# A decoder layer's opening stage: one norm block's parts and the next one's scaling in a fixed order, and other banks for even blocks

## The chip, the cores and the metric

The kernel runs on one core of a Trainium2 chip. The metric is device time in microseconds of one execution; the kernel before takes 1291.82 us (median of three runs, 1291.59 to 1291.99). The engines are named as in the profile: PE (TensorE, with PEld for its weight loads), DVE (VectorE), ACT (ScalarE), POOL (GpSimd) and SP (SyncE, which issues the DMAs here).

## The reference

One layer over 1040 tokens (16 meta tokens ahead of 1024) of width 1024, all in float32. What matters for the change is the beginning: RMSNorm of the input, then the combined input projection.

```python
h = jnp.concatenate([meta, x], axis=1)
a = rmsnorm(h, ln_mix_pre[l])            # h * rsqrt(mean(h*h) + 1e-6) * gain
proj = a @ w_in[l]
dq, dk, dv, hq, hf, hi, hg = jnp.split(proj, SPLITS, axis=-1)
```

Behind it come differential attention (four heads, two softmaxes each), HGRN2 (a gated linear recurrence), the output projection, a second norm and a feed-forward part with a short convolution. The change touches none of these.

## The kernel before, in words

Every matrix product is made of three: each operand is split into a high part (a cast to the rounded float32 that TensorE multiplies fast) and a low part (operand minus high part), and high times high, high times low and low times high are summed in PSUM.

**Norm blocks.** The tokens come in nine blocks of 128 rows (the last has 16). A block i goes through these steps:
- its rows are loaded into `xt` (`load_x`, four buffers, the first of which the gain row `grow` uses at the start);
- ACT squares them with a running sum into a score bank `pj` and makes the row factor `ss` with a logarithm and an exponential (`pre_stat`);
- DVE multiplies each half (512 columns) by the factor and the gains `gb` into `xs` (`pre_scale`, the SCALAR_TENSOR_TENSOR `xs<-xt,ss,gb`), here called scaling(i, half);
- PE transposes each half in four steps into a PSUM bank `px` (`pre_turn`, L292);
- ACT casts the bank to the high part (`pre_hi`, CAST `a<-px`) and DVE subtracts for the low part (`pre_lo`, TENSOR_TENSOR `a<-px,a`).

**PSUM.** Three tags have two buffers each: "ip" (one bank, the projections' sums `pi`), "m" (one bank, most transposes) and "S" (a pair of banks, the score tiles of attention, which the opening also uses). A transposition into an "m" bank waits until the low part of the half that had that bank is made. A projection's sum in an "ip" bank waits until the result before the last is evacuated: dv's first matmul waits for dq's evacuation, which is an ACT multiplication (`q<-pi_dq`) and then DVE's low part (`q<-pi_dq,q`, two instructions).

**Tokens and weights.** The projections of head 0 (dq, dk, dv) run over three token groups; the first needs blocks 0 and 1, the second blocks 2 to 4, the third blocks 5 to 8. Weights come in halves of 512 rows of the contraction. For dq and dk, ACT casts a half and POOL subtracts for its low part; for dv (tile `w`, called `third` in the code), DVE casts and POOL subtracts. Raw halves go through three buffers `wr`, so a fourth load waits until POOL has read the first.

**What sets the order.** PE's instructions stand as they are written. In the opening, ACT's and DVE's do too, as long as `state["ordered"]` is true (class `Ordered`): each instruction issued through `A` or `V` keeps its place in the program. After that a scheduler places them. SP's DMAs stand in one queue: a load that waits holds up those behind it. Norm work and projection are mixed by `interleave`: its side generator (`pre_blocks`) yields after each half block, and between two yields the dense generator gives PE a budget of matmuls; `lead` is the budget ahead of the first.

The ordered part ends, before, with block 2's scaling. Block 2's transposes and parts, block 3's scaling and dv's two casts follow in the scheduler's order.

## Time and profile before

| | |
|---|---|
| median of three runs | 1291.82 us (1291.59 to 1291.99) |
| the profiled execution | 1290.12 us |
| its span, first to last instruction | 1288.3 us |
| mean granted clock of PE | 0.997 |
| PE, DVE, ACT, POOL busy | 98%, 70%, 54%, 32% of the span |

The profile describes one execution. A row of its order in time gives start and duration in us, the engine, the line, the operation, the tile written and the tiles read; a bracket at the end gives the idle time of the engine before it and what ended that. Rows of many ACT and DVE instructions carry L57, the line of the helper that records them, so they are told apart by their tiles. Names are without numbers: `px` stands for all the transposes' banks. "x4" joins four equal instructions. The opening with the change ends at about 45 us.

### The profile page before, as it was taken

What the parts mean: (1) busy time and instruction counts of PE and PEld (TensorE: products, weight loads), DVE (VectorE), ACT (ScalarE), POOL (GpSimd) and SP (SyncE); (2) the same over time, 40 slices, a digit from 0 to 9 for tenths busy, and PEclk for the clock granted to TensorE, in tenths of its full rate; (3) what the DMA queues carried; (4) which work ended last, traced back from release to release, by engine and by line L of the source; (5) the groups of instructions that cost most, each with busy time, mean ns of one, the idle gap of its engine ahead of it and who ended that gap; (6) DMA issues with size and microseconds to landing.
All of it is one profiled execution on the core that took longest, in us unless ns stands there. A gap on an engine that the chain in (4) does not pass through costs nothing.

```text
span 1288.3 us, 26390 instructions
## 1 busy us (share of the span) xinstructions
PE 1268.2 (98%) x10264; PEld 1181.5 (92%) x10264; DVE 904.2 (70%) x1579; ACT 692.1 (54%) x1698; POOL 409.4 (32%) x322
## 2 busy tenths in 40 slices
PE   7999999999999999999999999999999999999997
PEld 7899999999999999777999999999999998888886
DVE  6576647564757476747797778778778786697587
ACT  7465357545654566446665445445445454454454
POOL 3221212021212110122165766766766730010120
PEclk9999999999999999999999999999999999999999
DMA  6222222212222223837512322222222237955363
GB/s 223 95 84 69 84 83 98 70 68 83 99 73 89 66 91 110 269 104 241 204 59 84 112 77 91 75 83 90 76 83 85 81 101 233 340 185 172 90 213 123
DMA packets 84387, 153.07 MB, mean 119 GB/s; under 512 B 9587, under 2 KB 19859, under 8 KB 84262
## 3 DMA queue, kind: packets, MB, share of 16 engines
q1 hardware_dynamic: 84262, 151.39, 35.4%
q8 instruction: 80, 1.31, 0.4%
q14 instruction: 45, 0.37, 0.1%
HBM read 112.69 MB, written 38.67 MB: 117 GB/s over the span
## 4 chain that ended last, share of the span: by engine, by line
PE 66%; DVE 2%; ACT 1%; DMA 0%; issue 0%; DVEq 0%
PE pd L1616 5%; PE pd L1615 5%; PE pd L1614 5%; PE pb L1415 4%; PE pb L1416 4%; PE pb L1417 4%; PE pa L1416 3%; PE pa L1417 3%; PE pa L1415 3%; PE pc L1416 3%; PE pc L1415 3%; PE pc L1417 3%; PE py L1030 2%; PE py L1034 2%; PE py L1032 2%; PE pq L1392 2%
## 5 line engine op out<-in xcount | busy, mean ns | idle before, releaser
L1415 PE MATMUL pb<-t,uh 128*128 128x258 f32 (+1 forms) x456 | 127.4, 279 | 0.6 <-DVE u L57 0.6
L1416 PE MATMUL pb<-t,uh 128*128 128x258 f32 (+1 forms) x456 | 127.3, 279 | 0.0
L1417 PE MATMUL pb<-t,ul 128*128 128x258 f32 (+1 forms) x456 | 127.2, 279 | 0.0
L1616 PE MATMUL pd<-wh,gl 128*128 128x512 f32 (+1 forms) x314 | 121.0, 386 | 0.0
L1615 PE MATMUL pd<-wl,gh 128*128 128x512 f32 (+1 forms) x314 | 120.5, 384 | 0.4 <-DVE wl L57 0.3
L1614 PE MATMUL pd<-wh,gh 128*128 128x512 f32 (+1 forms) x314 | 120.8, 385 | 0.0
L57 DVE SCALAR_TENSOR_TENSOR c<-uu,cwt,c 128x512 f32<-128x512 f32 x88 | 94.9, 1079 | 22.2 <-ACT c L57 21.4
L1364 POOL TENSOR_TENSOR c<-c,c 128x512 f32<-128x512 f32 x44 | 64.3, 1462 | 127.1 <-ACT c L57 112.9
L57 DVE SCALAR_TENSOR_TENSOR c<-ug,cwt,c 128x512 f32<-128x512 f32 x88 | 83.9, 954 | 6.6 <-ACT c L57 5.9
L1415 PEld LDWEIGHTS pb<-t,uh 128*128 128x128 f32 x456 | 85.8, 188 | 0.9 <-DVE u L57 0.8
L1416 PEld LDWEIGHTS pb<-t,uh 128*128 128x128 f32 x456 | 85.9, 188 | 0.0
L1417 PEld LDWEIGHTS pb<-t,ul 128*128 128x128 f32 x456 | 85.9, 188 | 0.0
L1416 PE MATMUL pa<-t,uh 128*128 128x256 f32 (+1 forms) x304 | 85.3, 281 | 0.0
L1417 PE MATMUL pa<-t,ul 128*128 128x256 f32 (+1 forms) x304 | 85.2, 280 | 0.0
L1415 PE MATMUL pa<-t,uh 128*128 128x256 f32 (+1 forms) x304 | 85.2, 280 | 0.0
L1417 PE MATMUL pc<-t,ul 128*128 128x256 f32 x304 | 83.9, 276 | 0.0
L1415 PE MATMUL pc<-t,uh 128*128 128x256 f32 x304 | 83.9, 276 | 0.0
L1416 PE MATMUL pc<-t,uh 128*128 128x256 f32 x304 | 83.9, 276 | 0.0
L1615 PEld LDWEIGHTS pd<-wl,gh 128*128 128x128 f32 x314 | 58.9, 188 | 14.0 <-DVE wl L57 1.5
L1616 PEld LDWEIGHTS pd<-wh,gl 128*128 128x128 f32 x314 | 59.0, 188 | 12.1
L1614 PEld LDWEIGHTS pd<-wh,gh 128*128 128x128 f32 x314 | 59.0, 188 | 11.6
L57 ACT ACTIVATE c<-ug,cbt,cwt 128x512 f32<-128x512 f32 x44 | 35.9, 817 | 44.0 <-issue 26.2
(421 smaller groups left out, 4278.2 us busy)
## 6 DMA issues: line engine op xcount, KB each, us to landing
ra<-in_wup_dram SPq DMA_DIRECT2D x76, 256.0 KB, 2.7
wd<-in_wdown_dram SPq DMA_DIRECT2D x44, 256.0 KB, 3.3
tsc<-wd SPq DMA_DIRECT2D x44, 256.0 KB, 2.5
gsc<-c SPq DMA_DIRECT2D x44, 256.0 KB, 2.0
wi<-tsc SPq DMA_DIRECT2D x44, 256.0 KB, 2.9
gi<-gsc SPq DMA_DIRECT2D x33, 256.0 KB, 4.0
wi<-in_wdown_dram SPq DMA_DIRECT2D x33, 256.0 KB, 3.7
msc<-mm SPq DMA_DIRECT2D x21, 256.0 KB, 3.6
```

Source lines behind the costliest of these rows:

```text
L57: ins = call(*args, **kw)
L1030: T.matmul(py[:r], mh[:, j, :r], hi, start=(first and j == 0), stop=False)
L1032: T.matmul(py[:r], mh[:, j, :r], lo, start=False, stop=False)
L1034: T.matmul(py[:r], ml[:, j, :r], hi, start=False, stop=(last and k == k1 - 1))
L1364: G.tensor_tensor(cg, cg, cu, op=ALU.mult)
L1392: T.matmul(pt, hi[:, s], th[:, k], start=(kh + k == 0), stop=False)
L1415: T.matmul(pt, hi[:, s], th[:, k], start=(first and k == 0), stop=False, skip_group_check=True)
L1416: T.matmul(pt, hi[:, s], tl[:, k], start=False, stop=False, skip_group_check=True)
L1417: T.matmul(pt, lo[:, s], th[:, k], start=False, stop=(k == 3), skip_group_check=True)
L1614: T.matmul(py, gh[:, s], wh, start=(k == 0 and pr not in (3, 7)), stop=False, skip_group_check=True)
L1615: T.matmul(py, gh[:, s], wl, start=False, stop=False, skip_group_check=True)
L1616: T.matmul(py, gl[:, s], wh, start=False, stop=(k == NH - 1), skip_group_check=True)
```

## The change

It does five things, all in the opening:
- the load of block 3 is issued ahead of the second half of dk's weights;
- block 2's transposes, high and low parts, dv's two casts with POOL's two subtractions, and block 3's scaling are written into the ordered part, with the matmuls that PE has between them;
- block 3's `xs` is made there, so `pre_block(3)` finds it ready;
- even blocks that remain (4, 6 and 8) transpose both halves into one pair of the "S" tag, instead of two "m" banks;
- the load of block 6 is issued by itself ahead of the interleaving, which now begins with block 3 and a lead of 700 instead of 2600.

```diff
@@ pre_block
         for half in range(2):
-            out_ = pre_turn(i, half, xs[:, 512 * half:])
+            if i % 2 == 0 and half == 0:
+                pair = ps_s(f"px{i}")
+            out_ = pre_turn(i, half, xs[:, 512 * half:], None if i % 2 else pair[:, half])
             pre_hi(*out_)
@@ opening
     keep_warm(4)
+    load_x(3)
     raws[1, 1] = load_raw(tiles[1][0], 1, tiles[1][1])
-    load_x(3)
     scale(0, 1)
@@ end of the ordered part
     scale(2, 1)
+    third = [ap_.tile([P, 4, 512], F32R, tag="pb", name=f"w3{c}", bufs=2) for c in range(2)]
+
+    def third_weights(c):
+        V.tensor_copy(third[c][:, 0], raws[2, c])
+        G.tensor_tensor(third[c][:, 1], raws[2, c], third[c][:, 0].bitcast(F32), op=ALU.subtract)
+
+    parts.append([(third[c][:, 0], third[c][:, 1]) for c in range(2)])
+    xss[3, 0] = zp.tile([P, D], F32, tag="xs", name="xs3")
+    xss[3, 1] = xss[3, 0][:, 512:]
+    for _ in range(22):
+        next(first_group)
+    h20 = pre_turn(2, 0, xss[2, 0])
+    third_weights(0)
+    scale(3, 0)
+    pre_hi(*h20)
+    pre_lo(*h20)
+    for _ in range(8):
+        next(first_group)
+    h21 = pre_turn(2, 1, xss[2, 1])
+    last_hi = pre_hi(*h21)
+    third_weights(1)
+    pre_lo(*h21)
+    scale(3, 1)
     xts.pop(2)
+    xts.pop(3)
     state["ordered"] = False
-    third = [ap_.tile([P, 4, 512], F32R, tag="pb", name=f"w3{c}", bufs=2) for c in range(2)]
-    parts.append([])
-    for c in range(2):
-        raw = raws[2, c]
-        with tc.issue_after(V.last.ins):
-            V.tensor_copy(third[c][:, 0], raw)
-            G.tensor_tensor(third[c][:, 1], raw, third[c][:, 0].bitcast(F32), op=ALU.subtract)
-        parts[2].append((third[c][:, 0], third[c][:, 1]))
@@ after the definitions
-    interleave(first_group, [pre_blocks([2, 3, 4])], 800, 2600)
+    load_x(6)
+    interleave(first_group, [pre_blocks([3, 4])], 800, 700)
```

On DVE, from block 2's second scaling (`xs_267`) to dq's low parts: a minus is a row of before, a plus one of the change. `xs_344` and `xs_283` are block 3's, `w_281` and `w_282` dv's two halves, `px_0` and `px_1` block 2's transposed halves, and `a_109` the low parts.

```order
 L57 SCALAR_TENSOR_TENSOR xs_267<-xt_154,ss_251,gb 128x512
-L57 SCALAR_TENSOR_TENSOR xs_344<-xt_219,ss_276,gb 128x512
 L57 CAST w_281<-wr_dv_0_235 128x512
-L57 SCALAR_TENSOR_TENSOR xs_344<-xt_219,ss_276,gb 128x512
+L57 SCALAR_TENSOR_TENSOR xs_283<-xt_217,ss_276,gb 128x512
+L57 TENSOR_TENSOR a_109<-px_0_306,a_108 128x4x128
 L57 CAST w_282<-wr_dv_1_244 128x512
-L57 TENSOR_TENSOR a_109<-px_0_310,a_108 128x4x128
 L57 TENSOR_TENSOR a_109<-px_1_324,a_108 128x4x128
+L57 SCALAR_TENSOR_TENSOR xs_283<-xt_217,ss_276,gb 128x512
 L57 SCALAR_TENSOR_TENSOR q_0_133<-pi_dq_0_162,q_0_133 64x256
 L57 SCALAR_TENSOR_TENSOR q_0_134<-pi_dq_0_162,q_0_134 64x256
```

Dv's first cast now stands ahead of scaling(3, 0), block 2's first low part ahead of the second cast, and scaling(3, 1) behind the second low part; dq's low parts stay behind all of it.

On ACT, from block 3's factor (`ss_276`) on: `px_0` and `px_1` are again block 2's halves, `pj_384` and `ss_385` block 4's squares and factor, `pj_459` block 5's squares.

```order
 L57 ACTIVATE ss_276<-ss_276 128x1
+L57 CAST a_108<-px_0_306 128x4x128
+L57 CAST a_108<-px_1_324 128x4x128
 L57 ACTIVATE pj_384,ss_385<-xt_222 128x1024
-L57 CAST a_108<-px_0_310 128x4x128
-L57 CAST a_108<-px_1_324 128x4x128
-L57 ACTIVATE ss_385<-ss_385,eps 128x1
 L57 ACTIVATE q_0_133<-pi_dq_0_162 64x256
 L57 ACTIVATE q_0_134<-pi_dq_0_162 64x256
-L57 ACTIVATE ss_385<-ss_385 128x1
-L57 ACTIVATE pj_459,ss_460<-xt_246 128x1024
```

Block 2's high parts moved ahead of block 4's squares, and block 4's factor behind dq's evacuation.

In SP's queue, at the second half of dk's weights (`wr_dk_1`): `xt_154` is block 2's load, `xt_219` and `xt_217` block 3's, `xt_222` block 4's.

```order
 L270 DMA xt_154<-in_x_dram 128x1024
-L810 DMA wr_dk_1_217<-in_win_dram 128x512
-L270 DMA xt_219<-in_x_dram 128x1024
+L270 DMA xt_217<-in_x_dram 128x1024
+L812 DMA wr_dk_1_219<-in_win_dram 128x512
 L270 DMA xt_222<-in_x_dram 128x1024
```

Block 3's load and dk's second half changed places; block 4's stays behind both.

## The prediction

> **What bounds the kernel now.** I read the page first, then the waits of TensorE (PE), then the order of time on each engine around the longest wait. The page says that PE is busy nearly throughout:

> ```profile
> span 1288.3 us, 26390 instructions
> ...
> PE 1268.2 (98%) x10264; PEld 1181.5 (92%) x10264; DVE 904.2 (70%) x1579; ACT 692.1 (54%) x1698; POOL 409.4 (32%) x322
> ```

> So a gain at one place stays if PE is then earlier for good. The waits of PE (total us, times, longest) have one long one:

> ```profile
> PE px L292 <- DVE a L57: 3.0, 1, 3.0
> ...
> PE pb L360 <- DVE a L57: 0.4, 1, 0.4
> ```

> The change touches the stage of the 3.0. On PE, in order of time (start us, us):

> ```profile
> 18.25 0.28 PE L896 MATMUL pi_dk<-a,wh_dk 128*128 128x256 f32 x1
> 21.51 0.82 PE L292 MATMUL px<-ident,xs 128*128 128x128 f32 x4 [2.98 <-DVE a L57]
> 21.99 0.99 PE L896 MATMUL pi_dk<-a,wh_dk 128*128 128x256 f32 x3
> 23.07 0.55 PE L249 MATMUL pi_dv<-a,w 128*128 128x256 f32 x1
> ...
> 28.34 0.34 PE L249 MATMUL pi_dq<-a,wh_dq 128*128 128x384 f32 x1
> ```

> Block 3's first transposes (21.51) stand in PE's queue ahead of ready matmuls. They write a bank of the pair "m" that block 2's first half still holds until its low part (DVE `a<-px,a`) is made. DVE makes that late:

> ```profile
> 15.33 1.60 DVE L57 SCALAR_TENSOR_TENSOR xs<-xt,ss,gb 128x512 f32<-128x512 f32 x1
> 17.71 0.75 DVE L57 SCALAR_TENSOR_TENSOR xs<-xt,ss,gb 128x512 f32<-128x512 f32 x1 [0.77 <-ACT ss L57]
> 18.38 0.42 DVE L57 CAST w<-wr_dv 128x512 fp32r<-128x512 f32 x1
> 18.71 0.74 DVE L57 SCALAR_TENSOR_TENSOR xs<-xt,ss,gb 128x512 f32<-128x512 f32 x1
> 19.37 1.48 DVE L57 CAST w<-wr_dv 128x512 fp32r<-128x512 f32 x1
> 20.78 1.27 DVE L57 TENSOR_TENSOR a<-px,a 128x512 fp32r<-128x512 f32 x2
> 22.07 0.86 DVE L57 SCALAR_TENSOR_TENSOR q<-pi_dq,q 64x256 fp32r<-64x256 f32 x2
> ```

> (In order: scaling(2,1), scaling(3,0), dv's first cast, scaling(3,1), its second cast, block 2's two low parts, the two q parts.) Two are longer than their kind: a scaling takes 0.75 but here 1.60, a cast 0.42 but here 1.48. Beside them POOL ran:

> ```profile
> 15.10 1.29 POOL L160 TENSOR_TENSOR wl_dk<-wr_dk,wh_dk 128x512 fp32r<-128x512 f32 x1 [0.96 <-ACT wh_dk L57]
> 18.87 1.70 POOL L924 TENSOR_TENSOR w<-wr_dv,w 128x512 fp32r<-128x512 f32 x1 [2.48 <-DVE w L57]
> 20.94 1.28 POOL L924 TENSOR_TENSOR w<-wr_dv,w 128x512 fp32r<-128x512 f32 x1 [0.36 <-DVE w L57]
> ```

> The scaling of 15.33 ends 0.54 after POOL's 16.39; the cast of 19.37 ends 0.28 after POOL's 20.57; POOL's own 1.70 began while the scaling of 18.71 ran. So DVE scalings and casts out of SBUF and POOL's subtractions exclude each other; the low parts, which read PSUM, do not.

> The stall has a second price. In stretches of one clock record, 3.41 us each (PE busy is the first number behind the comma, PEclk the third from the right, then DMA share and GB/s):

> ```profile
> 18.45:21.87 3.42, 0.44 (x4) 0.36 (x4) 3.42 (x6) 3.38 (x10) 2.63 (x2) 1.00 0.94 336
> 21.87:25.28 3.41, 3.31 (x16) 3.05 (x15) 3.32 (x7) 2.26 (x7) 0.35 (x1) 0.50 0.31 81
> 602.13:605.55 3.42, 2.75 (x14) 1.93 (x13) 3.42 (x4) 2.17 (x7) 1.50 (x1) 1.00 0.76 225
> 1281.39:1284.80 3.41, 0.49 (x5) 0.28 (x3) 3.25 (x7) 1.81 (x7) 0.00 (x0) 1.00 0.68 266
> 1284.80:1288.21 3.41, 0.00 (x0) 0.00 (x0) 0.58 (x1) 0.00 (x0) 0.00 (x0) 0.50 0.49 181
> ```

> A stretch with PE busy 0.44 or 0.49 of 3.41 us is followed by one at half clock. At 2.75 of 3.42 the kernel kept its clock.

> **The change part by part.** *Block 3's load ahead of dk's second half.* SP and ACT, before:

> ```profile
> 4.36 0.43 SPq L270 DMA_DIRECT2D xt<-in_x_dram  x1
> 11.21 0.33 SPq L810 DMA_DIRECT2D wr_dk<-in_win_dram  x1
> 11.64 0.85 SPq L270 DMA_DIRECT2D xt<-in_x_dram  x2
> ```
> ```profile
> 14.40 0.62 ACT L57 CAST wh_dk<-wr_dk 128x512 fp32r<-128x512 f32 x1
> 15.96 1.03 ACT L57 ACTIVATE pj<-xt 128x1024 f32<-128x1024 f32 x1 [0.94 <-DMA xt<-in_x_dram]
> ...
> 17.47 0.20 ACT L57 ACTIVATE ss<-ss 128x1 f32<-128x1 f32 x1
> ...
> 19.92 0.76 ACT L57 ACTIVATE q<-pi_dq 64x256 fp32r<-64x256 f32 x2
> ```
> ```profile
> 14.00:15.00 1.00, 1.00 (x10) 1.00 (x10) 0.94 (x2) 1.00 (x3) 0.14 (x1) 1.00 1.10 373
> 11.00:12.00 1.00, 1.00 (x8) 1.00 (x7) 1.00 (x2) 0.86 (x3) 1.00 (x2) 1.00 0.01 4
> ```

> The weight load at 11.21 had to wait for POOL; block 3's load stood behind it. Now that load goes out about 0.45 after 4.36, and the DMA engines that sat idle at 11 to 12 have it to move. The 0.94 before ACT's squares goes, and block 3's factor is ready at 17.67 - 1.0 = 16.7. Price: its 0.5 MB takes 1.4 us at 373 GB/s, estimated. It costs the weights nothing if it stays behind those issued ahead of it, up to 1.4 if it shares with them; I take nothing, since everything ahead is issued by then and it joins the end. The same 1.4 us are gained by dv's weights behind it: landed by 18.38 before, by 17.0 now (estimate; bounds 15.6, with the idle us and the start-up gained too, and 18.4).

> *The fixed order on DVE.* From scaling(2,1), whose end stays at 16.93:
> - dv's first cast 17.0 to 17.4, scaling(3,0) to 18.1 (0.75), block 2's first low part to 18.7 (half of 1.27).
> - Block 3's transposes start at 18.75, not 21.51: the 2.98 falls to about 0.4. PE then does three dk matmuls and is through at 19.6.
> - POOL's first subtraction, begun at 17.5, takes 1.70 beside a scaling as it did before: to 19.2. The second cast ends 0.28 later, 19.5; the second low part at 20.1.
> - POOL's second subtraction runs 19.55 to 20.85. Scaling(3,1), ready at 20.0, is now behind it: 20.85 + 0.54 = 21.4. Before, it was done at 19.45.
> - Queued behind it on DVE are the two q parts: 0.86, to 22.25.

> **What is late next** is those q parts. The first dv matmul takes the bank that dq's result leaves only then (there are two such banks). Before: parts done 22.93, matmul 23.07, 0.14 later. Now 22.25 + 0.14 = 22.4. PE waits 19.6 to 22.4, 2.8 us: the stall moves behind the transposes. Gain at this point 23.07 - 22.4 = 0.7.

> [...]

> *From the first dv matmul to 28.34*, where the second token group starts. In 18.45 to 21.87 PE now works 18.75 to 19.6 and the first 0.1, about 0.95 of 3.41 (28%). Whether that halves the clock is unmeasured: the bounds are 14% (halved) and 80% (not), and 28% is nearer the first. If halved, the slow stretch holds 25.28 - 22.4 = 2.9 us of work instead of 2.2, and each costs half: 0.35 of the 0.7 is lost, and the gain is about 0.4. If not, 2.2 / 2 = 1.1 more is gained: 1.8. DVE, busy over 97% of both rows, has block 4's scalings behind all this, so I take 1.7.

> *The pair of score banks* takes even blocks' waits for an "m" bank away. The only such wait of note was block 3's, which is odd: nothing here, and 0.4 at block 8 (the pb row) is the wait for the low part itself. Bounds: 0 and -0.4. *The fixed order on ACT* (block 2's high parts ahead of block 4's squares) is what gives the low part at 18.7; it costs nothing: the squares and the two high parts stood ahead of the q evacuation of 19.92 before as well, and block 3's factor, ahead of all three, is 1.0 earlier. Without that it would be the second low part that waits, and DVE is not at it before 19.4. *Later loads.* Block 7's load waits for scaling(3,1), now 21.4, behind three small tables on SP, where before the three of blocks 5 to 7 were out by 19.84:

> ```profile
> 14.54 5.30 SPq L270 DMA_DIRECT2D xt<-in_x_dram  x3
> ```
> ```profile
> 27.63 1.02 ACT L57 ACTIVATE pj<-xt 128x1024 f32<-128x1024 f32 x1
> ```

> Block 7's squares ran at 27.63: 6 us of cover. Without it, 1.9 us of delay would fall on block 7's transposes.

> Sum on the profiled execution: span 1288.3 - 0.4 = 1287.9, and the 1.8 around it (its time was 1290.12) gives 1289.7. That execution was 1.7 under the median of the runs, 1291.82; taken from the median, the forecast is 1291.4.

> **The rivals.**
> 1. *The clock stays up.* 28% busy suffices. For: nothing halved at 80%. Against: 13 and 14% did. Gain 1.7: 1290.1. [...]
> 2. *Slower: dv's weights land late.* The first cast now stands ahead of scaling(3,0) and the low part in fixed order, so every us of landing past 17.0 moves all of it. At the present landing, 18.4, dv's first matmul starts at 23.8, 0.7 later than now, and 0.35 of that comes back since less work falls into the slow stretch: 0.4 of loss, 1292.2. It decides from 17.7, where the 0.7 is used up. For: the cast at 18.38 started just when DVE and the weights allowed. Against: SP issues the same transfers earlier.
> 3. *The exclusion does not bite*: POOL's second subtraction starts after scaling(3,1). Then scaling(3,1) ends at 20.75, the q parts at 21.6, dv's first matmul starts at 21.75, 1.3 earlier; with the clock kept (1.1) and block 4's scalings earlier too (0.6) the gain is 3.0: 1288.8. Against: POOL began 0.1 after each cast before. The upper bound is stall and slow clock both gone, 3.0 + 1.7 = 4.7.

> **How the numbers follow.** Forecast 0.48, rival 1 0.27, rival 2 0.17, rival 3 0.08. The range 1289.7 to 1292.6 holds the forecast and rivals 1 and 2 with 0.4 of slack for the landing's bounds, and leaves out rival 3 and the tails. A measurement can tell 0.2%, 2.6 us, from no change. Only rival 3 passes it below: its 0.08, and 0.02 for what I don't see. Above, only rival 2 with more going wrong, 0.05. Within: 0.85.

> **What would show it.** Right: the wait of px for DVE `a` falls under 0.7, and a wait of 2 to 3 us stands before the first pi_dv matmul, at 22.4; one scaling of 1.3 us ends at about 21.4; PEclk 0.50 in 21.87 to 25.28. Wrong: dv's first matmul before 21.5 or after 23; a cast of w that waits for a DMA; or a new PE wait after 28 us, which would mean that the gain is not kept.

## The result, and the profile after

The changed kernel is slower: 1292.43 us (median of 22 executions, 1290.87 to 1298.29) against 1291.33 us for the kernel before beside it (22 executions, 1289.95 to 1294.35). The ratio is 1.0015, 95% interval [1.0009, 1.0022], so 0.15%, about 1.9 us; the two medians alone lie 1.1 us apart. The forecast was 0.4 us faster.

The profiled execution took 1293.35 us with a span of 1291.5, that is 3.2 more than the span before (1288.3). It lay 0.9 over its own median, and that of before 1.2 under the median of its 22. So the two profiles show more than the change costs as a rule, and the 3.2 is taken apart here with that in mind.

The waits of PE after (us in total, times, longest), the lines that answer to those of before:

```profile
PE pi_dv L249 <- DVE q L57: 2.7, 1, 2.7
...
PE px L292 <- DVE a L57: 1.0, 2, 0.6
...
PE pl L494 <- issue: 0.8, 1, 0.8
```

Of the 3.0 ahead of block 3's transposes 0.44 is left, and 2.7 stands before dv's first matmul. The line of `px` now holds two short waits, this one and one of 0.60 at block 8. The line of `pl` is new: a wait in which no semaphore is waited for. In order of time on PE:

```profile
19.23 0.66 PE L292 MATMUL px<-ident,xs 128*128 128x128 f32 x4 [0.44 <-DVE a L57]
19.64 0.60 PE L898 MATMUL pi_dk<-a,wh_dk 128*128 128x256 f32 x3
22.92 0.55 PE L249 MATMUL pi_dv<-a,w 128*128 128x256 f32 x1 [2.68 <-DVE q L57]
...
30.01 0.33 PE L249 MATMUL pi_dq<-a,wh_dq 128*128 128x384 f32 x1
...
46.87 0.41 PE L292 MATMUL px<-ident,xs 16*128 16x16 f32 x4 [0.60 <-DVE a L57]
47.14 0.89 PE L362 MATMUL pb<-oh,tbb 32*128 32x384 f32 x2
...
533.63 0.35 PE L494 MATMUL pl<-mix,kr 128*32 128x16 f32 x20 [0.78 <-issue]
```

Read against before: dv's first matmul is 0.15 earlier (22.92 for 23.07), but the second token group starts 1.67 later (30.01 for 28.34). So in this execution the first part of the loss comes between 23 and 30 us. The matmul `pb` behind block 8 ran at 44.90 in the kernel before:

```profile
44.90 0.91 PE L360 MATMUL pb<-oh,tbb 32*128 32x384 f32 x2 [0.35 <-DVE a L57]
```

It is 2.24 later now, so another 0.57 went between 30 and 47 us. The last 1.0 came in one piece at 533 us. The sum is 1.67 + 0.57 + 1.0 = 3.2; of the 1.67, 0.26 was there before the change's first wait (scaling(2,1) ends at 17.19, not 16.93).

DVE and POOL after, from scaling(2,1) on:

```profile
15.59 1.60 DVE L57 SCALAR_TENSOR_TENSOR xs<-xt,ss,gb 128x512 f32<-128x512 f32 x1
17.48 0.43 DVE L57 CAST w<-wr_dv 128x512 fp32r<-128x512 f32 x1 [0.29 <-DMA wr_dv<-in_win_dram]
17.82 0.75 DVE L57 SCALAR_TENSOR_TENSOR xs<-xt,ss,gb 128x512 f32<-128x512 f32 x1
18.48 0.69 DVE L57 TENSOR_TENSOR a<-px,a 128x512 fp32r<-128x512 f32 x1
19.08 0.91 DVE L57 CAST w<-wr_dv 128x512 fp32r<-128x512 f32 x1
19.91 0.68 DVE L57 TENSOR_TENSOR a<-px,a 128x512 fp32r<-128x512 f32 x1
20.51 1.37 DVE L57 SCALAR_TENSOR_TENSOR xs<-xt,ss,gb 128x512 f32<-128x512 f32 x1
21.91 0.86 DVE L57 SCALAR_TENSOR_TENSOR q<-pi_dq,q 64x256 fp32r<-64x256 f32 x2
...
25.62 0.69 DVE L57 TENSOR_TENSOR a<-px,a 128x512 fp32r<-128x512 f32 x1 [0.58 <-ACT a L57]
26.23 0.74 DVE L57 SCALAR_TENSOR_TENSOR xs<-xt,ss,gb 128x512 f32<-128x512 f32 x1
27.97 0.69 DVE L57 TENSOR_TENSOR a<-px,a 128x512 fp32r<-128x512 f32 x1 [0.99 <-ACT a L57]
```
```profile
17.98 1.72 POOL L922 TENSOR_TENSOR w<-wr_dv,w 128x512 fp32r<-128x512 f32 x1 [1.35 <-DVE w L57]
20.07 1.27 POOL L922 TENSOR_TENSOR w<-wr_dv,w 128x512 fp32r<-128x512 f32 x1 [0.36 <-DVE w L57]
```

Scaling(3,1) stands at 20.51 with 1.37: POOL's second subtraction ends at 21.34, and it ends 0.54 later, at 21.88, as forecast. The q parts follow, and dv's first matmul 0.15 after them. The gaps of 0.58 and 0.99 at the end are DVE waiting for high parts of transposes that PE makes at half clock (the four at 23.91 and the four at 26.25 took 1.05 us each, the four at 19.23 took 0.66 at full clock). In stretches of one clock record (the columns as in the prediction):

```profile
18.70:22.11 3.41, 1.10 (x8) 0.81 (x7) 3.38 (x5) 3.34 (x9) 2.28 (x2) 1.00 0.49 164
22.11:25.53 3.42, 2.61 (x12) 2.64 (x13) 2.84 (x6) 1.11 (x5) 0.00 (x0) 0.50 0.69 208
25.53:28.94 3.41, 3.41 (x17) 3.21 (x16) 2.04 (x3) 2.70 (x6) 0.00 (x0) 0.50 0.25 56
```

There are two stretches at half clock in a row, where the kernel before had one. The first begins with the rest of dv's wait, so PE is busy only 2.61 of 3.42 in it, and a second one follows. Before, PE was busy 3.31 of 3.41 in the slow stretch, and full clock came back behind it.

The stretches begin at other places in each execution (at 18.45 in the profile of before, at 18.70 here, at 20.27 in g2), and that decides how a stall falls into them. g2_after_shift2 and e10_shift (below) are the changed kernel with one and four small matmuls more at its start, and the same order on DVE and ACT. In both nearly the whole wait falls into one stretch, one stretch at half clock follows and is busy throughout, and the second token group starts at 28.37 and 29.03, not at 30.01. g2's rows:

```profile
20.27:23.68 3.41, 1.24 (x11) 1.26 (x12) 3.32 (x6) 2.83 (x10) 0.59 (x1) 1.00 0.42 102
23.68:27.10 3.42, 3.42 (x18) 3.27 (x16) 2.89 (x5) 2.90 (x6) 0.00 (x0) 0.50 0.53 176
```

A second slow stretch then came in both, at 47.58 and at 48.01, behind block 8. So each of these three executions has two slow stretches by 52 us, where the profiled execution of the kernel before has one; that the two stand in a row is a matter of this execution.

### The profile page after: what moved, and what is told of

It is laid out like the page before. It is cut to its first block, busy times and chain, and to the rows that moved or that the text cites. A ratio compares the mean times of both kernels' runs of the same rounds, so it can differ in the third digit from the quotient of the medians.

```text
span 1291.5 us, 26389 instructions
## 1 busy us (share of the span) xinstructions
PE 1269.8 (98%) x10264; PEld 1182.4 (92%) x10264; DVE 905.7 (70%) x1579; ACT 692.7 (54%) x1698; POOL 411.8 (32%) x322
## 3 DMA queue, kind: packets, MB, share of 16 engines
q8 instruction: 80, 1.31, 0.4%
## 4 chain that ended last, share of the span: by engine, by line
PE 65%; DVE 2%; ACT 1%; DMA 0%; issue 0%; DVEq 0%; ACTq 0%
PE pd L1634 5%; PE pd L1635 5%; PE pd L1633 5%; PE pb L1434 4%; PE pb L1435 4%; PE pb L1436 4%; PE pa L1435 3%; PE pa L1434 3%; PE pa L1436 3%; PE pc L1434 3%; PE pc L1435 3%; PE pc L1436 3%; PE py L1049 2%; PE py L1053 2%; PE py L1051 2%; PE pq L1411 2%
## 5 line engine op out<-in xcount | busy, mean ns | idle before, releaser
L57 DVE SCALAR_TENSOR_TENSOR c<-uu,cwt,c 128x512 f32<-128x512 f32 x88 | 93.8, 1066 | 22.3 <-ACT c L57 21.4
L57 DVE SCALAR_TENSOR_TENSOR c<-ug,cwt,c 128x512 f32<-128x512 f32 x88 | 84.0, 955 | 6.6 <-ACT c L57 5.9
L1258 POOL TENSOR_TENSOR ws<-ra,ra 128x512 f32<-128x512 f32 x38 | 57.0, 1501 | 8.4 <-DMA ra<-in_wup_dram 5.6
```

Of the source, the lines that this page charges most:

```text
L57: ins = call(*args, **kw)
L1258: G.tensor_tensor(sums[nm], a, b, op=op)
```

## The experiments

Theory A is the clock: the moved stall brings a second slow stretch. Theory B is the pair: in blocks 4, 6 and 8 the second half's transposes wait for the first half's low part. The rival is the prediction's own step, by which the pair costs nothing and one slow stretch comes as before. The ratio is to the kernel before on the same chip; the granted clock is the mean over the kernel's executions. Over 112 executions of the kernel before it was 0.9979, and over 22 of the changed kernel 0.9974. A step of 0.001 in it is, estimated from a time of 1291 us and the 0.50 of the record, 2.6 us at half clock, or 1.3 us of PE's work. So as a rule the lost clock is 0.0005, an estimated 0.65 us of PE's work, of the 1.9 us. A clock of 0.996 or less stood in 5 of the 22 executions of the changed kernel and in 5 of the 112. By the two profiles that is two slow stretches or more beside the one at the end: that of before has one beside it and 0.997, that after two and 0.996.

| run | ratio [95%] | clock |
|---|---|---|
| the changed kernel | 1.0015 [1.0009, 1.0022] | 0.9974 |
| e1_no_pair | 1.0011 [1.0002, 1.0021] | 0.9971 |
| e2_pair_only | 1.0033 [1.0021, 1.0045] | 0.9970 |
| e3_after_warm | 1.0008 [0.9998, 1.0018] | 0.9983 |
| e5_reorder | 1.0015 [1.0006, 1.0023] | 0.9972 |
| e7_before_warm | 1.0014 [1.0004, 1.0023] | 0.9988 |
| e8_warm_no_pair | 1.0006 [0.9997, 1.0015] | 0.9988 |
| e10_shift | 1.0019 [1.0008, 1.0031] | 0.9970 |
| e11_q_first | 1.0020 [1.0011, 1.0029] | 0.9975 |
| f1_before_warm28 | 0.9990 [0.9982, 0.9999] | 0.9988 |
| f2_load | 1.0000 [0.9991, 1.0009] | 0.9978 |
| f3_load_warm24 | 0.9987 [0.9979, 0.9996] | 0.9988 |
| g1_load_warm24_shift | 0.9990 [0.9980, 1.0000] | 0.9991 |
| g2_after_shift2 | 1.0009 [1.0000, 1.0018] | 0.9975 |

### The pair alone, and the change without it

e2_pair_only, on the kernel before:

```diff
-            out_ = pre_turn(i, half, xs[:, 512 * half:])
+            if i % 2 == 0 and half == 0:
+                pair = ps_s(f"px{i}")
+            out_ = pre_turn(i, half, xs[:, 512 * half:], None if i % 2 else pair[:, half])
```

> The kernel before with the pair of score banks for even blocks, and nothing else. Theory B: 0.7 us slower than before or a little more (blocks 4, 6, 8 wait for a low part; block 2's does not hold block 3 any more in the same bank). Theory A, and the prediction's step: within 0.3 us of before, since the stall of 2.98 us ahead of block 3 and its one slow stretch stay.

Measured: 1.0033, some 4 us slower. The order in time on PE shows block 2's second half:

```profile
21.93 1.12 PE L292 MATMUL px<-ident,xs 128*128 128x128 f32 x4 [4.06 <-DVE a L57]
```

In the kernel before, these transposes ran at 17.08 without a wait. In this run the first half's low part ends at 21.87, 0.06 ahead of them. The two halves now write one tile, and the second half's transposes wait until the first half's low part has read it, although they fill the other bank. Theory B holds in its direction and was too low in size: where the low part is late, the price is that lateness. The pair does the reverse of setting the halves free. It also brought early slow stretches in this run (half clock from 19.93 to 26.76). The scheduler's order on DVE changed with the pair as well: block 4's two scalings now stand ahead of dq's two q parts. So the 0.33% is the pair together with what the scheduler made of it.

e1_no_pair, on the changed kernel:

```diff
-            if i % 2 == 0 and half == 0:
-                pair = ps_s(f"px{i}")
-            out_ = pre_turn(i, half, xs[:, 512 * half:], None if i % 2 else pair[:, half])
+            out_ = pre_turn(i, half, xs[:, 512 * half:])
```

> The changed kernel, with even blocks' transposes back in the bank "m" (the fixed order stays). Theory A (the loss is the clock: two stretches of 3.41 us at half clock in a row instead of one, about 1.7 us): no change against the changed kernel, about 1.1 us (0.08%) over the kernel before or more. Theory B (the pair costs: in blocks 4, 6 and 8 the second half's transposes wait for the first half's low part, 0.2 + 0.25 + 0.6, less the 0.35 that block 8 waited before): 0.7 us faster than the changed kernel, those three waits gone. Both may hold, so that 0.7 of the loss goes and the rest stays. By the prediction's own step (the pair costs nothing) the waits go and nothing is gained.

Measured: 1.0011 for 1.0015; medians 1292.51 and 1292.43. The three waits are gone from the trace, and two slow stretches came early (25.01 to 31.84). The scheduler also put a low part ahead of block 4's scalings on DVE, and PE now waits 1.26 us for one of these at 27.16, so e1 differs in more than the pair. The difference has the sign of theory B, but the intervals overlap, so this pair of times decides nothing; that most of the loss stays without the pair fits theory A.

### The clock alone

f1_before_warm28, on the kernel before, puts dummies into the stall; they add zeros to dk's sum:

```diff
+                        if half and step == 2 and j == 1 and k == 4:
+                            for _ in range(28):
+                                T.matmul(pi[1][:, :P], zeros, zeros, start=False, stop=False, skip_group_check=True)
                         yield 115.0
```

> The kernel before with 28 small matmuls of zeros in the stall of 2.98 us, as in the run with 52; with 28 the order on every engine stays that of before (with 52 VectorE had taken two scalings of block 5 ahead of low parts of block 4). Theory A: no 0.50 in the first 40 us, and what the half clock costs the kernel before stands alone. TensorE would be 1.7 us earlier at the second token group, but VectorE is busy nearly without a gap from 15 to 28 us; what it can give is its own idle time there, the 0.9 us before block 4's first low part. So the second token group starts 0.9 us earlier than 28.34, and 0.5 to 1.0 us below the kernel before. If only the waits count and the clock is free, no change.

Measured: 0.9990 [0.9982, 0.9999], about 1.2 us faster, with useless work added. Its medians are 1290.66 and, of the kernel before beside it, 1291.83. The granted clock rose from 0.9977 (the 29 executions of before beside it) to 0.9988, worth an estimated 1.4 us of PE's work. The stretch that held the stall, and the next:

```profile
20.73:24.15 3.42, 2.44 (x26) 2.09 (x24) 3.36 (x7) 3.23 (x9) 1.56 (x2) 1.00 0.67 184
24.15:27.56 3.41, 3.30 (x28) 2.89 (x27) 3.33 (x6) 3.33 (x9) 0.00 (x0) 1.00 0.22 54
```

At full clock PE is no longer what DVE waits for: DVE is busy 3.33 of 3.41 in the second. So the clock has a price of its own, and DVE caps what comes back. The second token group started at 28.27, only 0.1 before 28.34, but this execution was already 1.1 us late ahead of the stall (scaling(2,1) ended at 18.03, not 16.93), with full clock from 13.91 and not from 11.63. The order did not stay the same, though the expectation had it so: on DVE a scaling of block 4 and one of block 5 moved one place up, so a part of the gain may be theirs.

e7_before_warm had 52 dummies in the same place:

```diff
-                            for _ in range(28):
+                            for _ in range(52):
```

> The kernel before, with 52 small matmuls of zeros added into dk's accumulation just ahead of the place where TensorE waits 2.98 us for block 3's transposes; they add zero to the sum, and nothing else is moved. Theory A (the clock has a price of its own: half clock follows a stretch with TensorE little busy, and costs 1.7 us for each stretch of 3.41 us): the record shows no 0.50 in the first 40 us, and the second token group starts 1.3 to 1.7 us earlier, at 26.7 to 27.0 instead of 28.34, although the stall stays as long as it was; 1.3 to 1.7 us below the kernel before at the end. Theory B (only the waits count): no change, within 0.3 us.

Measured: 1.0014, slower, though the clock was kept (0.9988). The order shows a likely reason. With 52 the scheduler, it seems, holds PE to be late, and puts two scalings of block 5 ahead of low parts of block 4 on DVE. DVE's rows:

```profile
23.11 1.42 DVE L57 SCALAR_TENSOR_TENSOR xs<-xt,ss,gb 128x512 f32<-128x512 f32 x2
24.58 0.69 DVE L57 TENSOR_TENSOR a<-px,a 128x512 fp32r<-128x512 f32 x1
25.19 0.74 DVE L57 SCALAR_TENSOR_TENSOR xs<-xt,ss,gb 128x512 f32<-128x512 f32 x1
25.98 0.86 DVE L57 TENSOR_TENSOR kl<-pi_dk,k 64x256 fp32r<-64x256 f32 x2
26.87 0.69 DVE L57 TENSOR_TENSOR a<-px,a 128x512 fp32r<-128x512 f32 x1
```

The scaling at 25.19 is block 5's. It stands ahead of block 3's second low part (26.87), whose bank block 4's second transposes need, and these waited 0.90. So the run was no clean test of the clock. It suggests that DVE's order in 23 to 29 us is worth as much as the clock; nothing here shows it by itself.

e3_after_warm, on the changed kernel:

```diff
+        warm = ps_s("warm")
+        for _ in range(44):
+            T.matmul(warm[:, 0, :P], zeros, zeros, start=True, stop=True)
         yield from proj_group(0, parts[2], tiles[2][1], tiles[2][2])
...
     third_weights(1)
+    stat[4] = pre_stat(4)
     pre_lo(*h21)
```

The line on `stat[4]` keeps ACT's order near the changed kernel's.

> The changed kernel with 44 small matmuls of zeros put on TensorE just ahead of dv's first matmul, where it waits 2.7 us for the q parts; their result is not used. Theory A: the stretch 18.70 to 22.11 is then over 80% busy, the clock is not halved at 22.11, and the time is 3.4 us below the changed kernel's if the dummies fit into the wait, 2 to 3 us if they overrun it a little. Theory B: the wait is filled with work of no use and the clock does not matter for the end: no gain, or a loss by the overrun.

Measured: 1.0008 [0.9998, 1.0018], some 0.9 us under the changed kernel and not the 2 to 3.4 that theory A gave; the intervals overlap. No half clock stood at 22 us, and the second token group started at 28.24, not 30.01. Then a slow stretch came where the changed kernel's own profile had none:

```profile
43.55:46.96 3.41, 2.81 (x18) 1.92 (x17) 2.15 (x10) 0.91 (x4) 0.00 (x0) 1.00 0.00 0
46.96:50.38 3.42, 3.42 (x13) 3.28 (x12) 0.38 (x1) 0.78 (x3) 0.21 (x1) 0.50 0.19 62
```

PE is busy in all of the second row, so it lost an estimated 1.7 us of work there (half of 3.42). The first row holds block 8's split transposes and their wait:

```profile
45.13 0.41 PE L292 MATMUL px<-ident,xs 16*128 16x16 f32 x4 [0.60 <-DVE a L57]
```

e8_warm_no_pair is the same without the pair:

```diff
-            if i % 2 == 0 and half == 0:
-                pair = ps_s(f"px{i}")
-            out_ = pre_turn(i, half, xs[:, 512 * half:], None if i % 2 else pair[:, half])
+            out_ = pre_turn(i, half, xs[:, 512 * half:])
...
+        warm = ps_s("warm")
+        for _ in range(44):
+            T.matmul(warm[:, 0, :P], zeros, zeros, start=True, stop=True)
...
     third_weights(1)
+    stat[4] = pre_stat(4)
     pre_lo(*h21)
```

> The changed kernel with both: the 44 small matmuls of zeros ahead of dv's first matmul, and even blocks' transposes back in the bank "m". In the run with the 44 alone the gain at 28 us was 2.1 us, and all but 0.2 us of it was lost at 47 us, where a stretch of 3.41 us that held block 8's split transposes with their wait of 0.6 us was followed by one at half clock. Theory C (the pair's wait at block 8 can cost a slow stretch of its own, on top of 0.7 us of waits): no 0.50 at 47 us, and 2 to 3 us below the changed kernel, 0.5 to 1 us below the kernel before. If the slow stretch at 47 us had nothing to do with the pair, it comes again, and the gain over the 44 alone is 0.7 us.

Measured: 1.0006 [0.9997, 1.0015], no half clock from 12 us until PE's work ends, and the second token group at 27.48. It is the fastest form of the changed kernel, 0.09% under it with overlapping intervals, but it is not below the kernel before, where theory C had it 0.5 to 1 us below. Of the six profiled executions with the pair (the changed kernel, e2, e3, e5, e10, g2), five have a slow stretch that begins between 46.9 and 50.7 us; of the nine without it none has. So the pair can cost more than its waits: 0.6 us of waits and, in these profiled executions, mostly a slow stretch. Over all 11 executions each, e3's clock is 0.9983 and e8's 0.9988, which is 0.4 of a slow stretch on the mean.

### The order on DVE, and the load

e5_reorder, on the changed kernel:

```diff
     h20 = pre_turn(2, 0, xss[2, 0])
-    third_weights(0)
     scale(3, 0)
     pre_hi(*h20)
     pre_lo(*h20)
+    scale(3, 1)
+    third_weights(0)
...
-    third_weights(1)
     pre_lo(*h21)
-    scale(3, 1)
+    for _ in range(6):
+        next(first_group)
+    third_weights(1)
...
-    interleave(first_group, [pre_blocks([3, 4])], 800, 700)
+    interleave(first_group, [pre_blocks([3, 4])], 800, 10)
```

> The changed kernel with the fixed order changed: scaling(3,1) ahead of dv's first cast, the second cast after the second low part. It takes the scaling out from behind the second subtraction on POOL. If the q parts' lateness by that exclusion (scaling(3,1) ending 0.54 after POOL) is what sets dv's first matmul at 22.9, it starts 1 to 1.5 us earlier, and by theory A one or both slow stretches go as well: 1 to 4 us below the changed kernel. If something else sets it (dv's own low weights, made later now), it starts no earlier and the time stays or rises by up to 1 us.

Measured: 1.0015, no change. dv's first matmul came only 0.6 earlier:

```profile
22.28 0.36 PE L249 MATMUL pi_dv<-a,w 128*128 128x256 f32 x1 [2.09 <-DVE q L57]
```

The second cast now stood between scaling(3,1) and the q parts and took over its part. One early slow stretch stood here and one at 47.68. g2 and e10 have the same pattern with the changed kernel's order, so it is not the reordering's doing.

e11_q_first, on e1_no_pair, puts the q parts ahead of scaling(3,1):

```diff
     pre_lo(*h21)
+    for _ in range(8):
+        next(first_group)
     scale(3, 1)
...
-    interleave(first_group, [pre_blocks([3, 4])], 800, 700)
+    interleave(first_group, [pre_blocks([3, 4])], 800, 10)
```

> The changed kernel without the pair, and with the q parts ahead of scaling(3,1) on VectorE (block 3's second scaling is what was shut out by GpSimd's subtraction and ended 0.54 us behind it, with the q parts queued behind). If that exclusion set dv's first matmul at 22.9, it now starts at 21.5 to 21.8; the stretch before it is then about 45% busy instead of 32%, and by theory A the slow stretches may go too: 1 us below the kernel before with the clock kept, level with it if one slow stretch stays. If the q parts wait for ScalarE's evacuation instead, dv's first matmul stays after 22.5 and nothing is gained over the changed kernel without the pair.

Measured: 1.0020, slower than the change without the pair. PE's waits and the stretches:

```profile
22.61 0.36 PE L249 MATMUL pi_dv<-a,w 128*128 128x256 f32 x1 [1.77 <-DVE q L57]
...
26.96 0.97 PE L292 MATMUL px<-ident,xs 128*128 128x128 f32 x4 [2.15 <-DVE xs L57]
```
```profile
20.27:23.68 3.41, 1.64 (x15) 1.47 (x13) 2.95 (x6) 3.34 (x10) 1.33 (x2) 1.00 0.45 122
23.68:27.10 3.42, 1.27 (x12) 1.09 (x11) 2.68 (x6) 3.38 (x10) 0.00 (x0) 1.00 0.64 197
```

The wait ahead of dv fell to 1.77 and its stretch (1.64 busy) kept the clock. But block 4's scaling came later by what had been put ahead of it, PE waited 2.15 for that, and this second stretch (1.27 busy) lost the clock instead. The stall moved once more.

f2_load, on the kernel before:

```diff
+    load_x(3)
     raws[1, 1] = load_raw(tiles[1][0], 1, tiles[1][1])
-    load_x(3)
```

> The kernel before with one part of the change alone: block 3's load ahead of dk's second weight load. Scaling(3,0) does not wait 0.77 us for its factor any more; VectorE is 0.5 to 0.8 us earlier from there. By the prediction's step on the load (it costs the weights nothing): 0.3 to 0.8 us below the kernel before, with dk's second weights no later. If the load holds up dk's weights, ScalarE's cast of them and GpSimd's subtraction come later by up to 1.4 us, dk's last matmuls wait, and it is slower.

Measured: 1.0000 [0.9991, 1.0009]. No gain. dv's first matmul ran at 22.23 (0.8 earlier), and then the same as in e11 happened. The edit moved more than the load: the scheduler answered with another order on DVE, in which scaling(3,1) stands behind the q parts, as in e11, and block 4's scalings run from 25.59, where the kernel before has them at 22.96 and 24.35:

```profile
26.48 0.95 PE L292 MATMUL px<-ident,xs 128*128 128x128 f32 x4 [2.06 <-DVE xs L57]
```

### The stop without a semaphore

At 533 us PE stands still for 0.78 us in the changed kernel, inside a run of very short matmuls (`pl`), waiting for no semaphore. The instructions of PE in the traces can be counted (weight loads, matmuls and semaphore waits, from 0). By the number of the first weight load behind it, every such stop in `pl` or `py` of 0.2 us or more stands at one of four places, to within one. From 2754 to 7618 it is 4864 instructions, 19 times 256, from there to 9922 it is 2304, 9 times 256, and 10177 is 255 further, so the remainder by 256 is the same:

| run | at us | instruction | remainder by 256 |
|---|---|---|---|
| the changed kernel | 533.6 | 9922 | 194 |
| e2, e5, e10 | 536.8, 533.9, 534.1 | 9922 | 194 |
| e3, e7, f3 | 161.3, 159.7, 159.2 | 2754, 2754, 2753 | 194, 194, 193 |
| e1, e10, f2 | 410.5, 409.9, 409.7 | 7618, 7617, 7617 | 194, 193, 193 |
| f3 | 536.0 | 10177 | 193 |

e10_shift and g2_after_shift2 are the changed kernel with a longer run-up:

```diff
-    keep_warm(20)
+    keep_warm(24)      # e10_shift; 21 in g2_after_shift2
```

> The changed kernel with four more small matmuls of zeros among the 20 at its start, where TensorE waits for the tables anyway: eight more instructions in TensorE's program and nothing else. The changed kernel lost 0.8 us at 533 us to a wait (pl, ended by issue) in which no semaphore was waited for; the same instruction showed it in two of the three experiments with the pair, 0.7 and 1.1 us, and none of it stood in the kernel before, whose program for TensorE has two instructions more. Theory D (it is the reading of TensorE's program, and depends on where in it the dense short matmuls of pl fall): the wait at this instruction goes or moves to another, 0.8 us below the changed kernel or no change. If it belongs to the data of that stage it stays at the same instruction.

> The changed kernel with one more small matmul of zeros among the 20 at its start: two more instructions in TensorE's program (a weight load and a matmul), as many as the change took out of it (two semaphore waits). Theory D (TensorE stops where a block of 256 instructions of its program begins inside the dense short matmuls of pl and was asked for too late): the blocks now begin where they do in the kernel before, which had no such stop, and the 0.78 us at 533 us is gone; 0.5 to 0.8 us below the changed kernel, the rest of the loss stays. If the stop belongs to the stage's data or to chance, it stays at 533 us or comes elsewhere at a place that is not number 194 of 256.

Measured: 1.0019 and 1.0009, neither told from the changed kernel. The stop stayed at number 9922 in both. In e10 that is a place in `pl` four matmuls earlier than in the changed kernel, in g2 one earlier, with 1.24 us of wait:

```profile
534.20 0.35 PE L494 MATMUL pl<-mix,kr 128*32 128x16 f32 x21 [1.24 <-issue]
```

So the stop is bound to the number in the program and not to the data of the stage: half of theory D holds. The other half falls: g2 has the kernel before's length, and there the trace has no stop at 9922. The DMA packets in the traces show what ends a stop. Each block comes by one transfer of 16 KB (80 of them for 20,619 instructions of PE, 258 each, in the changed kernel), and in all 13 stops (those of the table, g1's and g2's) PE went on 1.27 to 1.50 us after such a transfer had ended: in the changed kernel the transfer ended at 532.22 and PE went on at 533.63. In the kernel before, the transfer of the same block ended at 528.06, 2.35 us before the block began at 530.41, and PE did not stop. So a stop is a wait for a transfer that came late. What makes it late stays open. The stop at number 9922 stands in all five profiles with the pair and without small matmuls ahead of dv (the changed kernel, e2, e5, e10 and g2; 0.56 to 1.24 us) and in none of the four that have neither (the kernel before, e1, e11 and f2). So it may be part of the loss as a rule; by what way the change would bring it is not shown.

### A version that beats both

f3_load_warm24 is f2_load with the dummies of f1, 24 of them, and g1_load_warm24_shift has three more at the start:

```diff
+    load_x(3)
     raws[1, 1] = load_raw(tiles[1][0], 1, tiles[1][1])
-    load_x(3)
...
+                            for _ in range(24):
+                                T.matmul(pi[1][:, :P], zeros, zeros, start=False, stop=False, skip_group_check=True)
...
-    keep_warm(20)
+    keep_warm(23)      # g1 alone
```

> The kernel before with the earlier load and 24 small matmuls of zeros in the stall ahead of block 3's transposes: neither the pair nor the fixed order. If the load's gain on VectorE and the clock's price add, it is 0.8 to 1.6 us below the kernel before and the fastest so far. If VectorE's chain or a later stage takes it back, level with it.

> The kernel before with the earlier load, 24 small matmuls in the stall (the fastest so far, 0.9987), and three more at the start, so that its program for TensorE is as long as that of the kernel before with 28 in the stall, which showed no stop of this kind; without the three it showed two, 0.6 us in pl and 0.7 us in py. Theory D: both are gone, and it is 1.0 to 1.4 us faster than without the three: 0.9976 to 0.9980 of the kernel before. If the place in the program does not matter, 0.9987 again.

Measured: 0.9987 [0.9979, 0.9996] and 0.9990 [0.9980, 1.0000]. By these ratios f3 beats the kernel before by 1.7 us and, through it, the changed kernel by 0.28%; for g1 it is 1.3 us and 0.25%, with the interval's end at no change. f3's median lies only 0.7 us under that of the kernel before beside it (1291.14 and 1291.83), so the size is less sure than the sign. f3 is not told from f1 (0.9990), so the early load adds nothing that can be measured. In g1 the stop in `py` went and the one in `pl` stayed (0.4 us), and the time did not fall: the lengthening is no tool.

## Why the prediction was wrong, point by point

The median of 1292.43 lies inside the stated range of 1289.7 to 1292.6, beside the 1292.2 of the second rival. That is luck: the rival's weights did not land late enough, and the loss came by the two steps below that failed.

**The load, and dv's weights: right.** Block 3's squares ran at 15.18 (15.96 before), and its factor was there at 16.9. The first cast of dv stood at 17.48 instead of 17.0 and did wait for its DMA, 0.29, the sign that the prediction named. Its slower rival needed a landing past 17.7, and the cast ran before that.

**The stall moves to dv's first matmul: right in mechanism, 0.5 late.** Scaling(3,1) ended 0.54 behind POOL, the wait was 2.68, and `px` waited 0.44. The matmul came at 22.92 instead of 22.4; 0.26 of that is the start of this execution and 0.29 the cast's DMA. So 0.15 of the 0.7 was left.

**"If halved, the slow stretch holds 25.28 - 22.4 = 2.9 us of work ... 0.35 of the 0.7 is lost": the step that failed first.** The clock was halved, as forecast, but the sum assumed that the slow stretch ends by itself after 3.41 us. It did so where PE was busy nearly throughout (3.31 us of it in the kernel before, 3.33 in e5, 3.42 in g2). Here the moved stall reached 0.8 us into it, so PE was busy 2.61 of 3.42 and a second slow stretch followed. The forecast's own 2.9 us at half clock is, halved, an estimated 1.45 us of work, which is under the border found below (1.50 to 1.64): by that estimate the sum would have needed a second stretch even without the lateness of 0.5. In the profiled execution the second token group came 1.67 later instead of 0.4 earlier. The sum also laid the stall on the stretches of one execution. Where they begin elsewhere, as in g2 and e10, the second slow stretch comes at block 8 instead, and the second token group is 0.03 and 0.69 later than before. f1 shows the price nearly by itself: the one stretch of the kernel before is worth 0.10% [0.01, 0.18], with a small change of DVE's order in it. It was not had back in full: about 1.2 us of the estimated 1.7 that PE loses in the stretch, with DVE busy 3.33 of the next 3.41. "So I take 1.7", for the work of DVE behind it, stood in the prediction beside the right row, but the sum went on as if PE alone set 28.34.

**"The pair of score banks ... nothing here": the other step that failed.** It asked which waits the pair takes away, and not what it makes wait. e2 gives the sign (0.33% slower, with the scheduler's new order in it), and the trace of the changed kernel the size there: 0.57 us lost by 47 us, where block 8's 0.60 stands. In five of six profiled executions with the pair a slow stretch follows behind block 8. It is also the new wait of PE after 28 us that the prediction had named as a sign of being wrong.

**What the parts add up to.** Keeping the clock and taking the pair out (e8) brings the changed kernel from 1.0015 to 1.0006. So 0.09% of the 0.15% can be laid to these two together, with overlapping intervals; the split between them is not settled, since e1 and e3 differ from the changed kernel by less than their intervals. Nor is it settled whether anything of the loss remains: 1.0006 has the kernel before inside its interval. An estimate of the loss as a rule, from single numbers above, is 0.65 us for the clock, 0.57 for the pair's waits and 0.56 to 1.24 for the stop at 533 us: 1.8 to 2.5 for the measured 1.9; no run takes these away one by one. That the fixed order gains nothing is seen best in e8 beside f3. Both have the early load, small matmuls in the stall, no pair and the clock kept, and e8 alone has the fixed order: 1.0006 [0.9997, 1.0015] against 0.9987 [0.9979, 0.9996]. They ran on two chips and with 44 and 24 small matmuls, so how much it costs is open. That it saves a wait of PE in a stage that DVE sets is the reading that fits.

## What to carry to other kernels

A stall cost more than its length here where the clock was lost: the 2.68 us ahead of dv were followed by 6.83 us at half clock. So add up how busy the matmul engine is in each stretch of the clock's record, and ask of a stall that is moved which stretches it falls into, and whether the slow one is busy enough to end (3.31 of 3.41 us was, 2.61 was not). Ask it for other places of the stretches too, since they began elsewhere in each execution here (18.45, 18.70 and 20.27 us). Filling a stall with useless matmuls gave what no reordering here gave (0.9987 to 0.9990 in f1, f3 and g1, against 1.0015 in e5 and 1.0020 in e11), as long as the scheduler's order stayed nearly as it was (1.0014 in e7, where it did not). Two halves put into one tile were coupled here: the second half's writer waited for the first half's reader, 4.06 us in e2, though they lie in two banks.

## What the runs showed of the hardware

**One border for the clock.** At full clock, half clock followed stretches with PE busy 0.44, 1.10, 1.27 and 1.50 of 3.41 us, and did not follow 1.64 and 2.44; the 1.50 is e5's:

```profile
20.37:23.78 3.41, 1.50 (x13) 1.53 (x14) 3.24 (x6) 3.18 (x10) 1.87 (x2) 1.00 0.76 233
```

The 0.50 of the record is not quite half the speed for dv's matmuls of 256 columns: in the changed kernel's slow stretches they began 0.21 us apart (25.19, 25.40, 25.61), at full clock 0.12 (29.53, 29.65, 29.77). So the estimates above that take half of a slow stretch for lost are somewhat high for such matmuls. With 0.12 of 0.21 the 2.61 and 3.31 are 1.49 and 1.89, and the border still fits; the forecast's 2.9 is then 1.66, so whether its own slow stretch would have been the last stays open.

**The rounded float32.** In the profile of before, at full clock, matmuls of it with 384 columns began 0.17 us apart (dq's at 28.52, 28.69 and 28.86). The two of plain float32 with 384 columns, `pb` at 44.90, took 0.84 us to the next matmul at 45.74, 0.42 each.

**A program that is read in blocks.** The stops fall at one remainder of 256 (194 or 193), and the page of the changed kernel counts 80 transfers for 20,619 instructions of PE:

```profile
q8 instruction: 80, 1.31, 0.4%
```

That is 16 KB each (1.31 MB over 80), and 258 instructions, near the 256 of the places. The stops at these places, inside runs of short matmuls, took from 0.2, the least that the table counts, to 1.24 us. How short the matmuls are, by a row of the kernel before, 62 in 0.70 us:

```profile
530.07 0.70 PE L492 MATMUL pl<-mix,kr 128*32 128x16 f32 x62
```
